# Sample attention of a hybrid decoder trunk: whole cache loads with the newest row written over the oldest

## The chip, the cores and the metric

The kernel runs on one core of one Trainium2 chip. The metric is the device time of one execution in microseconds (us), and the median of several runs is what counts. A profile of one further execution is read beside it.

## What is computed

Two layers of a decoder trunk, for a prompt of 2048 tokens and for eight sample tokens that share the weights. Each layer normalizes its input, multiplies it by one wide matrix, runs three mixers on column groups of the result, and multiplies their outputs by one output matrix:

```python
u = _rmsnorm(x, norm_w) @ w_in
...
o, k1, v1 = _swa_decode(q, k, v, kc, vc, sinks)     # the sample tokens' attention
...
y = jnp.concatenate([ya, yb, yc], axis=-1) @ w_out
return x + y
```

The change is in the attention of the sample tokens. Each of the eight tokens has a cache of the last 128 keys and values (two heads of 64), and one new key and value. It sees the newest 128 rows, so all of the cache but its oldest row, and its own:

```python
def _swa_decode(q, k, v, kc, vc, sinks):
    kk = jnp.concatenate([kc, k], axis=1)
    vv = jnp.concatenate([vc, v], axis=1)
    s = jnp.einsum('nqhgd,nkhd->nhgqk', q.reshape(N, T, HK, G, Dh), kk) * (Dh ** -0.5)
    delta = (Wc + jnp.arange(T))[:, None] - jnp.arange(Wc + T)[None, :]
    s = jnp.where((delta >= 0) & (delta < WINDOW), s, -jnp.inf)
    p = _sink_softmax(s, sinks)
    o = jnp.einsum('nhgqk,nkhd->nqhgd', p, vv)
    return o, kk[:, -Wc:], vv[:, -Wc:]
```

The caches after the step (`s_k`, `s_v`) are outputs too. Scores, softmax and the weighted sum do not depend on the order in which the 128 rows stand, if keys and values stand in the same order.

## The kernel before

The prompt is worked through in blocks of 512 tokens, four in each layer. For each block the kernel multiplies by the input matrix in column groups (`g0`, `qk`, `v`, `o`, `z`, `x0`, `x1`, `cq`, `cz`, `bz`) and, between `z` and `x0`, by the output matrix for the block before. The unit of work is a chunk: 128 rows of weights by up to 512 columns, twelve matmuls on TensorE (`multiply`, lines 511 and 513: four token tiles, three products of high and low parts). In a layer's first block the weights are loaded raw, split in two parts and written back to DRAM; in later blocks a chunk loads the two parts ready made, 512 KB in one DMA (`load_chunk`, line 469, tile `hl` from `kept`; six buffers, issued four chunks ahead). All loads and stores are issued on SyncE's queue (SP), one behind the other.

Beside the matmuls run streams, Python generators that emit their next piece of work when a planner (`pump`, with a rate for each stream and a modelled clock) lets them between two chunks. The stream `d` is the sample tokens' work. `dec_1` is its part in the second block of each layer: gates, the mLSTM update and then the attention, `dec_c`. At the last chunk of `cq` what is left of `d` is emitted at once (`drain`). The framework that builds the program then fixes each engine's order from a simulated time line and places all waits; an instruction may stand far from where the code emits it.

`dec_c` works in eleven buffers of 128 x 516 floats, of which `U` names the last six. It loads gate, queries, keys and values of the eight tokens into `U[0]`, `U[1]` and `U[2]` (lines 1557 to 1559), normalizes and rotates keys and queries (lines 1571 to 1579, results in `U[4]` and `U[5]`), and stores them to a small DRAM tile `qd` (1582, 1583). The copies of the cache to the outputs go from DRAM to DRAM (1586), and the new row behind them (1589). Then `whole` loads K: the caches of four tokens go to one buffer, with cache row on the partition, in `U[0]` and `U[1]`. Cache rows 1 to 127 come in one DMA to partitions 0 to 126 (1598), the new row from `qd` in another one to partition 127 (1599). V goes to `U[4]` and `U[5]` in the same way, at the second of the eight tokens (1614). For each token the queries are broadcast to all partitions (1603, two buffers, loaded one token ahead), GpSimd multiplies them by the keys (1617), and VectorE sums over the head (1619). The scores of all tokens are transposed on TensorE (1625), and softmax, the transposed weights (1643), the products with V (1649) and the output's transposes (1658) follow.

Of the kernel before, what the change touches and what calls it, by code (L numbers as in the profile page):

```python
# [166 lines left out]
class Build:  # L167
# [1385 lines left out]
    def dec_c(self, l, L, D):  # L1553
        nc, I, O, U = self.nc, self.I, self.O, self.U[5:]
        TT = nc.vector.tensor_tensor
        y = self.s([8, 512], "dy")
        uz = self.load_us(l, 4368, 512, U[0])
        q = self.load_us(l, 3600, 512, U[1])
        kv = self.load_us(l, 4112, 256, U[2])
        k, v = kv[:, 0:128], kv[:, 128:256]  # L1560

        def v8(ap):
            return ap.rearrange("p (h c) -> p h c", c=64)

        R = self.rope_load(self.I['rope'][SEQ].partition_broadcast(8), 8)
        yield
        tabs = self.rope_tables(R, L, 8)
        self.dec_gate(l, 4368, y, uz, U[3], True)
        rs = yield from self.qk_norm(8, [q], k.unsqueeze(1), [U[i][:8, 0:512] for i in (4, 5)])
        yield  # L1570
        TT(v8(k), v8(k), rs[:, 8:10].unsqueeze(2).to_broadcast([8, 2, 64]), op=ALU.mult)
        sc = self.s([8, 8], "dsc")
        nc.vector.tensor_scalar(sc, rs[:, 0:8], 0.125, None, op0=ALU.mult)
        TT(v8(q), v8(q), sc.unsqueeze(2).to_broadcast([8, 8, 64]), op=ALU.mult)
        tm, kr, qr = [U[i][:8] for i in (3, 4, 5)]
        self.rope(8, v8(k), tabs[1], v8(kr[:, 0:128]), 2, v8(tm[:, 0:128]), nc.vector)
        nc.vector.tensor_copy(kr[:, 128:256], v)
        yield
        self.rope(8, v8(q), tabs[0], v8(qr[:, 0:512]), 8, v8(tm[:, 0:512]), nc.vector)
        qd = self.dr.tile([8, 768], F32, name=self.nm("qd"))  # L1580
        yield
        nc.sync.dma_start(qd[:, 0:512], qr[:, 0:512])
        nc.sync.dma_start(qd[:, 512:768], kr[:, 0:256])
        cat = "b w a d -> b w (a d)"
        for cache, out in (('cache_k', 's_k'), ('cache_v', 's_v')):
            nc.sync.dma_start(O[out][l, :, 0:127].rearrange(cat), I[cache][l, :, 1:128].rearrange(cat))
        yield
        for i, out in enumerate(('s_k', 's_v')):
            nc.sync.dma_start(O[out][l, :, 127].rearrange("b a d -> b (a d)"), qd[:, 512 + 128 * i:640 + 128 * i])
        ST = self.s([128, 64], "dST")  # L1590
        Ks, Vs = U[0:2], U[4:6]

        def whole(name, x, c0):

            for i in range(2):
                bs = slice(4 * i, 4 * i + 4)
                d = x[i][:, 0:512].rearrange("p (b c) -> p b c", b=4)
                nc.sync.dma_start(d[0:127], I[name][l, bs, 1:128].rearrange("b w a d -> w b (a d)"))
                nc.sync.dma_start(d[127:128], qd[bs, c0:c0 + 128].unsqueeze(0))  # L1599

        def load(b):
            qb = U[2 + b % 2][:, 0:512]
            nc.sync.dma_start(qb, qd[b, 0:512].partition_broadcast(128))
            return qb

        whole('cache_k', Ks, 512)
        nxt = load(0)
        yield
        for b in range(8):
            qb = nxt  # L1610
            if b < 7:
                nxt = load(b + 1)
            if b == 1:
                whole('cache_v', Vs, 640)
            kb = Ks[b // 4][:, (b % 4) * 128:(b % 4) * 128 + 128].rearrange("p (a d) -> p a d", d=64)
            q4 = qb.rearrange("p (a h d) -> p a h d", a=2, d=64)
            nc.gpsimd.tensor_tensor(q4, q4, kb.unsqueeze(2).to_broadcast([128, 2, 4, 64]), op=ALU.mult)
            yield
            nc.vector.tensor_reduce(ST[:, b * 8:b * 8 + 8], v8(qb), AX.X, ALU.add)

        SK = U[0][:, 0:64]
        nc.vector.tensor_copy(SK.rearrange("p (b h) -> p b h", h=8), L['sink'].unsqueeze(1).to_broadcast([128, 8, 8]))
        yield
        ps = self.mx()
        nc.tensor.transpose(ps[:64, 0:128], ST, self.ident)
        nc.tensor.transpose(ps[:64, 128:256], SK, self.ident)
        sk = self.s([64, 1], "dsk")
        nc.vector.tensor_copy(sk, ps[:64, 128:129])
        m, nm, es, den = [self.s([64, 1], f"dsm{i}") for i in range(4)]
        nc.vector.tensor_reduce(m, ps[:64, 0:128], AX.X, ALU.max)  # L1630
        TT(m, m, sk, op=ALU.max)
        TT(es, sk, m, op=ALU.subtract)
        nc.scalar.activation(es, es, AF.Exp)
        nc.vector.tensor_scalar(nm, m, -1.0, None, op0=ALU.mult)
        P = U[2][:64, 0:128]
        nc.scalar.activation(P, ps[:64, 0:128], AF.Exp, bias=nm, accum_out=den)
        yield
        TT(den, den, es, op=ALU.add)
        nc.vector.reciprocal(den, den)
        nc.vector.tensor_scalar(P, P, den, None, op0=ALU.mult)  # L1640
        yield
        pt = self.mx()
        nc.tensor.transpose(pt[:, 0:64], P, self.ident[:64, :64])
        PT = U[3][:, 0:64]
        nc.vector.tensor_copy(PT, pt[:, 0:64])
        yield
        po = self.mx()
        for b in range(8):
            nc.tensor.matmul(po[:, b * 8:b * 8 + 8], Vs[b // 4][:, (b % 4) * 128:(b % 4) * 128 + 128], PT[:, b * 8:b * 8 + 8],
                             start=True, stop=True)  # L1650
        oS = U[3][:, 64:96].rearrange("p (h b) -> p h b", b=8)
        p4 = po[:, 0:64].rearrange("p (b a h) -> p a h b", a=2, h=4)
        nc.vector.tensor_copy(oS[0:64], p4[0:64, 0])
        nc.vector.tensor_copy(oS[64:128], p4[64:128, 1])
        yield
        pf = self.mx()
        for h in range(4):
            nc.tensor.transpose(pf[:8, h * 128:h * 128 + 128], oS[:, h, :], self.ident)
        TT(y, y, pf[:8, :], op=ALU.mult)
        yield  # L1660
        self.dec_finish(y, 2, L)
        yield
# [225 lines left out]
```

## Time and profile before

| | us |
|---|---|
| median of 3 runs (3124.88 to 3131.53) | 3127.26 |
| the profiled execution | 3129.54 |
| its span, first to last instruction | 3127.7 |
| TensorE busy in the span | 2956.6 |
| VectorE busy | 1876.9 |
| ScalarE busy | 1252.6 |
| GpSimd busy | 713.0 |

The mean granted TensorE clock is 0.976 of full speed. PE is TensorE's matmuls, PEld its weight loads, DVE VectorE, ACT ScalarE, POOL GpSimd, and SPq the issuing of DMAs on SyncE. A row of a timeline gives start and duration of an instruction; the bracket at its end is the time for which its engine stood idle before it, and what ended that.

### The profile page before, as it was taken

The numbers are of one execution on the slowest core, as the hardware profiler recorded it, in microseconds if no ns is written. First come the engines' busy times: TensorE is split into PE (matmuls) and PEld (weight loads), VectorE is DVE, ScalarE is ACT, GpSimd is POOL, SyncE is SP. The second block draws the span as 40 slices with busy tenths as digits, with TensorE's granted clock in tenths as the row PEclk, the third lists the DMA queues.
The fourth block names the chain that finished last, engine by engine and source line by source line (L and its number), as shares of the span: only waits on it lengthen the run. The fifth ranks groups of instructions, "written<-read, shape, count | busy, mean of one in ns | idle before, by whom it ended". The sixth has DMA issues, their size and how long they took to land.

```text
span 3127.7 us, 42759 instructions
## 1 busy us (share of the span) xinstructions
PE 2956.6 (95%) x14722; PEld 2420.9 (77%) x14722; DVE 1876.9 (60%) x4630; ACT 1252.6 (40%) x3080; POOL 713.0 (23%) x808
## 2 busy tenths in 40 slices
PE   6999999699999999999999999996999999999988
PEld 5787878478777788887878778874888788878877
DVE  4259656377557664467644676572765658544774
ACT  4243545124633254323554344540255324442254
POOL 3336105122012310004331561231310204000300
PEclk9999999899999999999999999997999999999999
DMA  7865548365367555564565754574544764455533
GB/s 207 279 200 188 188 148 285 117 213 177 133 194 231 160 155 164 162 191 139 174 227 181 233 198 160 194 246 163 163 151 157 241 199 151 148 160 179 163 110 127
DMA packets 263685, 567.29 MB, mean 181 GB/s; under 512 B 66900, under 2 KB 100052, under 8 KB 263420
## 3 DMA queue, kind: packets, MB, share of 16 engines
q1 hardware_dynamic: 263468, 564.56, 56.0%
q8 instruction: 116, 1.90, 0.2%
q14 instruction: 101, 0.83, 0.1%
HBM read 434.70 MB, written 132.06 MB: 181 GB/s over the span
## 4 chain that ended last, share of the span: by engine, by line
PE 73%; DVE 9%; DMA 7%; SPq 3%; issue 3%; POOL 2%; ACT 2%; DVEq 0%; POOLq 0%; ACTq 0%
PE pj L511 31%; PE pj L513 26%; DMA wr<-in_w_in 2%; PE mx L1180 2%; PE mx L1143 2%; SPq L1599 2%; PE mx L974 2%; PE mx L1171 1%; DMA hl<-kept 1%; POOL hl L491 1%; DMA kept<-hl 1%; PE mx L533 1%; PE mx L534 1%; PE mx L1221 1%; PE mx L861 1%
## 5 line engine op out<-in xcount | busy, mean ns | idle before, releaser
L513 PE MATMUL pj<-hl,xTh 128*128 128x512 f32 (+1 forms) x3072 | 958.5, 386 | 14.9 <-DVE quad L554 6.8
L511 PE MATMUL pj<-xTh,hl 128*128 128x512 f32 x2240 | 735.2, 406 | 75.0 <-DMA hl<-kept 71.8
L513 PEld LDWEIGHTS pj<-hl,xTh 128*128 128x128 f32 x3072 | 567.5, 191 | 126.1 <-DVE quad L554 8.3
L513 PE MATMUL pj<-hl,xTl 128*128 128x512 f32 (+1 forms) x1536 | 585.5, 384 | 0.0
L511 PEld LDWEIGHTS pj<-xTh,hl 128*128 128x128 f32 x2240 | 425.9, 192 | 175.7 <-DMA hl<-kept 66.7
L511 PE MATMUL pj<-parts,hl 128*128 128x512 f32 x2016 | 517.5, 404 | 11.1 <-DVE parts L1235 4.1
L511 PE MATMUL pj<-xTl,hl 128*128 128x512 f32 x1120 | 441.8, 404 | 0.0
L511 PEld LDWEIGHTS pj<-parts,hl 128*128 128x128 f32 x2016 | 368.6, 189 | 91.7 <-DVE parts L1235 5.8
L491 POOL TENSOR_TENSOR hl<-wr,hl 128x512 fp32r<-128x512 f32 (+1 forms) x208 | 279.5, 1349 | 438.6 <-ACT hl L488 383.7
L513 PEld LDWEIGHTS pj<-hl,xTl 128*128 128x128 f32 x1536 | 292.7, 191 | 52.8
L511 PEld LDWEIGHTS pj<-xTl,hl 128*128 128x128 f32 x1120 | 214.5, 192 | 44.9
L1235 DVE SCALAR_TENSOR_TENSOR parts<-quad,lp_ynw,parts 128x512 fp32r<-128x512 f32 x168 | 141.7, 845 | 162.8 <-ACT quad L1232 74.7
L488 ACT ACTIVATE hl<-wr 128x512 fp32r<-128x512 f32 (+1 forms) x208 | 126.6, 615 | 232.2 <-DMA wr<-in_w_in 76.3
L1158 ACT ACTIVATE unit<-unit,c_m,c_sc 128x256 f32<-128x256 f32 (+1 forms) x192 | 112.2, 586 | 86.2 <-DVE c_m L1149 86.1
L1174 DVE TENSOR_TENSOR parts<-mx,parts 128x512 fp32r<-128x512 f32 x124 | 84.5, 686 | 96.6 <-ACT parts L1173 94.5
L649 DVE SCALAR_TENSOR_TENSOR quad<-quad,lp_cw,quad 128x512 f32<-128x512 f32 x192 | 142.0, 784 | 0.3
L1228 ACT ACTIVATE parts<-quad,lp_ynw 128x512 fp32r<-128x512 f32 x112 | 80.6, 722 | 152.2 <-PE pj L511 142.7
L1022 POOL TENSOR_TENSOR unit<-quad,rpqn 128x256 f32<-128x256 f32 x32 | 24.1, 755 | 503.5 <-PE mx L941 225.7
L1173 ACT ACTIVATE parts<-mx 128x512 fp32r<-128x512 f32 x124 | 73.1, 595 | 106.9 <-PE mx L1171 104.6
L1180 PE MATMUL mx<-parts,vs 128*128 128x512 f32 x248 | 104.0, 435 | 6.9 <-ACT parts L1173 5.6
L393 POOL TENSOR_TENSOR quad<-quad 128x512 f32<-128x512 f32 x24 | 33.6, 1399 | 296.9 <-ACT quad L391 296.3
L805 ACT ACTIVATE unit<-quad 128x128 f32<-128x128 f32 x128 | 39.8, 311 | 138.5 <-DVE quad L863 135.8
(404 smaller groups left out, 4562.8 us busy)
## 6 DMA issues: line engine op xcount, KB each, us to landing
hl<-kept SPq DMA_DIRECT2D x576, 512.0 KB
kept<-hl SPq DMA_DIRECT2D x192, 512.0 KB
wr<-in_w_in SPq DMA_DIRECT2D x144, 256.0 KB
hl<-kept SPq DMA_DIRECT2D x48, 272.0 KB
wr<-in_w_out SPq DMA_DIRECT2D x32, 256.0 KB
quad<-in_xT SPq DMA_DIRECT2D x32, 256.0 KB
x<-quad SPq DMA_DIRECT2D x32, 256.0 KB
quad<-x SPq DMA_DIRECT2D x16, 512.0 KB
```

The costliest lines, as they stand in the source:

```text
L488: nc.scalar.activation(h, raw, AF.Copy)
L491: nc.gpsimd.tensor_tensor(lw, raw, h.bitcast(F32), op=ALU.subtract)
L511: nc.tensor.matmul(ps[t], w[:, tt], a, start=st and first, stop=en and last)
L513: nc.tensor.matmul(ps[t][:, :N], a[:, tt], w[:, :N], start=st and first, stop=en and last)
L649: nc.vector.scalar_tensor_tensor(acc, u[:, j:j + 512], cw[:, j, c:c + 1], acc, op0=ALU.mult, op1=ALU.add)
L974: nc.tensor.matmul(pY[:, h * 64:h * 64 + 64], W[h // 4][:, (h % 4) * 128:(h % 4) * 128 + 128], xdt[:, h * 64:h * 64 + 64], start=True, sto ...
L1158: nc.scalar.activation(P(a, j), P(a, j), AF.Exp, bias=nm[:, j:j + 1], scale=head(sc, a, j), accum_out=den[:, j:j + 1])
L1173: nc.scalar.activation(PTh, pT, AF.Copy)
L1174: TT(PTl, pT, PTh.bitcast(F32), op=ALU.subtract)
L1180: nc.tensor.matmul(pO[a], vs[:, x, a, :], p, start=x == 0 and i == 0, stop=x == nk - 1 and i == 1)
L1228: nc.scalar.activation(yh.rearrange("p (t c) -> p t c", c=128), pt, AF.Copy, scale=L['ynw'][:, k:k + 1])
L1235: nc.vector.scalar_tensor_tensor(yl.rearrange("p (t c) -> p t c", c=128), blk, L['ynw'][:, k:k + 1], yh.bitcast(F32).rearrange("p (t c) -> ...
```

## The change

K's load moves ahead of the copies to the outputs, V's ahead of the first query's broadcast. Each load takes all 128 cache rows to the 128 partitions. The new row is written over the oldest one, on partition 0, by a DMA of its own: for K behind the copies' new rows, for V at the fourth token.

```diff
--- before.py
+++ after.py
@@ -1581,6 +1581,21 @@
         yield
         nc.sync.dma_start(qd[:, 0:512], qr[:, 0:512])
         nc.sync.dma_start(qd[:, 512:768], kr[:, 0:256])
+        Ks, Vs = U[0:2], U[4:6]
+
+        def whole(name, x):
+
+            for i in range(2):
+                d = x[i][:, 0:512].rearrange("p (b c) -> p b c", b=4)
+                nc.sync.dma_start(d, I[name][l, 4 * i:4 * i + 4].rearrange("b w a d -> w b (a d)"))
+
+        def newest(x, c0):
+
+            for i in range(2):
+                d = x[i][0:1, 0:512].rearrange("p (b c) -> p b c", b=4)
+                nc.sync.dma_start(d, qd[4 * i:4 * i + 4, c0:c0 + 128].unsqueeze(0))
+
+        whole('cache_k', Ks)
         cat = "b w a d -> b w (a d)"
         for cache, out in (('cache_k', 's_k'), ('cache_v', 's_v')):
             nc.sync.dma_start(O[out][l, :, 0:127].rearrange(cat), I[cache][l, :, 1:128].rearrange(cat))
@@ -1588,30 +1603,22 @@
         for i, out in enumerate(('s_k', 's_v')):
             nc.sync.dma_start(O[out][l, :, 127].rearrange("b a d -> b (a d)"), qd[:, 512 + 128 * i:640 + 128 * i])
         ST = self.s([128, 64], "dST")
-        Ks, Vs = U[0:2], U[4:6]
-
-        def whole(name, x, c0):
-
-            for i in range(2):
-                bs = slice(4 * i, 4 * i + 4)
-                d = x[i][:, 0:512].rearrange("p (b c) -> p b c", b=4)
-                nc.sync.dma_start(d[0:127], I[name][l, bs, 1:128].rearrange("b w a d -> w b (a d)"))
-                nc.sync.dma_start(d[127:128], qd[bs, c0:c0 + 128].unsqueeze(0))
 
         def load(b):
             qb = U[2 + b % 2][:, 0:512]
             nc.sync.dma_start(qb, qd[b, 0:512].partition_broadcast(128))
             return qb
 
-        whole('cache_k', Ks, 512)
+        newest(Ks, 512)
+        whole('cache_v', Vs)
         nxt = load(0)
         yield
         for b in range(8):
             qb = nxt
             if b < 7:
                 nxt = load(b + 1)
-            if b == 1:
-                whole('cache_v', Vs, 640)
+            if b == 3:
+                newest(Vs, 640)
             kb = Ks[b // 4][:, (b % 4) * 128:(b % 4) * 128 + 128].rearrange("p (a d) -> p a d", d=64)
             q4 = qb.rearrange("p (a h d) -> p a h d", a=2, d=64)
             nc.gpsimd.tensor_tensor(q4, q4, kb.unsqueeze(2).to_broadcast([128, 2, 4, 64]), op=ALU.mult)
```

## Rows read from the trace of the kernel before

**Rows 1.** Page, part 1: busy us, share of the span, instructions.

```profile
PE 2956.6 (95%) x14722; PEld 2420.9 (77%) x14722; DVE 1876.9 (60%) x4630; ACT 1252.6 (40%) x3080; POOL 713.0 (23%) x808
```

**Rows 2.** Waits of all engines: who for whom, total us, times, longest.

```profile
PE pj L511 <- DMA hl<-kept: 71.8, 9, 19.3
```

**Rows 3.** Stretches: us, busy (count) PE, PEld; then clock, DMA; L511 first.

```profile
580.00:640.00 60.00, 20.19 (x61) 14.09 (x60) 0.66 0.38 124
2096.00:2180.00 84.00, 47.36 (x164) 34.70 (x163) 0.78 0.39 132
...
580.00:640.00 60.00, 22.09 (x77) 16.46 (x76) 10.71 (x17) 6.52 (x20) 11.10 (x11) 0.66 0.38 124
2096.00:2180.00 84.00, 50.15 (x197) 39.14 (x196) 23.42 (x49) 8.01 (x29) 11.35 (x13) 0.78 0.39 132
```

**Rows 4.** Chain that ended last: start us, duration us, engine, line, count.

```profile
540.40 2.78 PE pj L511 x12
...
594.65 5.49 PE pj L511 x12
...
600.63 0.87 PE mx L853 x4
...
604.30 0.91 PE mx L861 x8
```

**Rows 5.** Timeline of SP: three of eight cache loads, the issue behind each.

```profile
560.70 0.26 SPq L1598 DMA_DIRECT2D unit<-in_cache_k  x1
561.28 10.57 SPq L469 DMA_DIRECT2D hl<-kept  x1
...
594.16 0.29 SPq L1598 DMA_DIRECT2D unit<-in_cache_v  x1
594.55 14.61 SPq L469 DMA_DIRECT2D hl<-kept  x1
...
2143.39 0.28 SPq L1598 DMA_DIRECT2D unit<-in_cache_v  x1
2143.72 13.16 SPq L1599 DMA_DIRECT2D unit<-qd  x1
```

**Rows 6.** DMA view, 560 to 576 us in 40 slices: GB/s.

```profile
GB/s 0 0 0 0 8 0 19 22 22 22 22 22 22 22 22 22 22 20 20 20 22 20 20 20 20 22 20 20 20 20 22 133 154 133 174 225 351 359 425 415
```

**Rows 7.** Timeline, layer 1: SP behind the first load, TensorE's next start.

```profile
2095.97 9.89 SPq L469 DMA_DIRECT2D hl<-kept  x1
...
2111.08 1.22 PE L511 MATMUL pj<-xTh,hl 128*128 128x512 f32 x2 [5.10 <-DMA hl<-kept]
```

**Rows 8.** Timeline, SSD state: its load on SP, the product that needs it.

```profile
889.86 0.38 SPq L1512 DMA_DIRECT2D unit<-in_state_ssm  x1
...
892.79 1.30 POOL L1525 TENSOR_TENSOR unit<-unit,ddA 128x512 f32<-128x512 f32 x1 [74.06 <-DMA unit<-in_state_ssm]
```

**Rows 9.** Waits of SP for DMAs: total us, times, longest.

```profile
SPq L1512 <- DMA out_s_h<-unit: 15.8, 9, 3.0
...
SPq L1603 <- DMA unit<-qd: 6.5, 5, 2.2
```

**Rows 10.** Timeline of SP, 60 to 100 us: the first output copy.

```profile
73.53 0.84 SPq L1586 DMA_DIRECT2D out_s_k<-in_cache_k  x1
```

**Rows 11.** Rotation's end, third sample, last sum, transposes: layer 0, then layer 1.

```profile
568.93 0.68 DVE L1025 TENSOR_TENSOR unit<-unit,unit 8x512 f32<-8x512 f32 x1
...
631.86 1.26 POOL L1617 TENSOR_TENSOR unit<-unit,unit 128x512 f32<-128x512 f32 x1 [30.88 <-DMA unit<-qd]
...
655.79 0.69 DVE L1619 TENSOR_REDUCE dST<-unit 128x8 f32<-128x512 f32 x1 [1.33 <-POOL unit L1617]
...
657.35 0.11 PE mx L1625
...
2104.89 0.67 DVE L1025 TENSOR_TENSOR unit<-unit,unit 8x512 f32<-8x512 f32 x1
...
2192.30 0.11 PE mx L1625
```

## The prediction

> **What bounds the kernel now.** I read the page first: TensorE is busy for 2956.6 us of the 3127.7 us span, 95% [rows 1], so time can be won or lost only where it stands or runs slowly. The view of waits says why it stands: nine waits of an output-projection or input-projection matmul (L511) for a kept weight tile, 71.8 us in all, the longest 19.3 us [rows 2]. The table by stretches shows that they lie in two places alone: from 580 to 640 us TensorE is busy for 22.09 us, so idle 37.9, and from 2096 to 2180 us for 50.15 us of 84, so idle 33.9; together these are the 71.8 [rows 3]. The granted clock there is 0.66 and 0.78, because after each standstill TensorE runs at 1.2 GHz for a while: twelve L511 matmuls take 5.49 us behind a wait and 2.78 us otherwise [rows 4]. These two stretches are where the sample tokens' attention of layer 0 and layer 1 loads its caches.
>
> What each stretch loses, idle time and slow clock together, is its length less its matmuls at full speed. One L511 matmul is 2.78/12 = 0.232 us; an L853 matmul 0.87/4 = 0.218; the others go by L861, 0.91/8 = 0.114 [rows 4]. First stretch: 61 x 0.232 = 14.1, 4 x 0.218 and 12 x 0.114 = 2.2, so 16.4 us of work in 60: **43.6 us lost**. Second: 164 x 0.232 = 38.0, 4 x 0.218 and 29 x 0.114 = 4.2, so 42.2 of 84: **41.8 us lost** [rows 3, 4]. Sum 85.4 us.
>
> Why the weights are late is seen on SP's queue. A load of 127 cache rows is issued in 0.26 to 0.29 us, and the DMA issue right behind it then lasts 10.57, 14.61 or 13.16 us where 0.3 to 0.4 is usual; there are eight such loads (two halves of K and of V in two layers), and these are the first, one of the middle and the last [rows 5]. During the first of them the whole core moves 20 to 22 GB/s [rows 6]: 254 KB at that rate is about 12 us, the length of the stall. So a load of 127 rows uses a small part of the DMA engines, and everything behind it on SP, the weights among it, stands until it has drained. How long TensorE lives on what was fetched before: the load of layer 1 blocks SP from 2095.97, and TensorE runs dry at 2111.08 - 5.10 = 2105.98, so some 10 us of cover [rows 7].
>
> **The change, part by part.**
>
> *128 rows in place of 127, eight loads.* The kernel has a transfer of this very shape: the SSD state, 128 partitions with four runs of 512 B. It is issued in 0.38 us at 889.86, and the GpSimd product that needs it starts at 892.79 [rows 8], so it lands within 2.9 us, with no stall behind it. With that, the eight stalls go, and with them up to 85.4 us. Bytes grow by 2 KB a load, which is nothing. What the trace leaves open is only that the source is the cache and not the state; both have runs of 512 B.
>
> The Trainium skill, page "DMA: Bandwidth & Descriptors", section "Why a DMA increments its semaphore by 16 and not by 1", says that the number of engines is the largest up to 16 that divides both sides' slowest dimension, with 127 partitions giving one engine. The 20 to 22 GB/s agree; the trace doesn't name the engine. By that rule the sum is the same 85.4, and the third and fourth cases below could not happen through the loads.
>
> *The newest row written over row 0, after the load.* Before, row 127 was a partition of its own and waited for nothing but the rotated values; now four small writes a layer must wait until the load that they overwrite has landed. They are the same count and size as before, so their issue costs nothing new. The wait is new, and SP holds it: behind it stand the weight loads, the query broadcasts and the block's stores. The trace has no such wait; its nearest are SP's waits for a store before a load, 3.0 us at most, and for the rotated values, 2.2 us at most [rows 9]. From below it is nothing (the V writes come three samples after their load); from above 4 x 3.0 = 12 us a layer. Against the 10 us of cover the excess is 2 us, and a restart at the slow clock costs 5.49 - 2.78 = 2.7 us more. I take nothing, since K's two halves share one landing, and keep 0 to 4.7 us a layer.
>
> The page's section "Two DMAs through the same engine are not ordered" speaks against this part: the second write of the same bytes must await the first's completion. No run here shows an overwriting DMA. With the page's fixed cost of about 2 us for one DMA (section "Anatomy of one DMA — SWDGE (gpsimd) path", another issue path) an estimate is 8 us a layer, under the cover, and the sum would not move.
>
> *K's load ahead of the copies to the outputs, V's ahead of the queries.* The copies are issued at 73.5 us, half a millisecond before the attention [rows 10]: the order in the code does not bind them, and being behind K's load costs nothing. K's first half was already issued at 560.70, ahead of the end of the rotation [rows 5]. V's load now stands ahead of the first query; V overwrites the buffers from which the rotated values are stored, so it waits for that store, which the first query waits for as well, and then takes two issues of 0.4 us. Cost: under 1 us a layer, covered by the same 10 us.
>
> *What is late next.* When weights come on time, TensorE reaches the transposes of the scores (L1625) sooner, and the scores have their own chain: query broadcast, product on GpSimd, reduction on VectorE, eight times over two buffers. Layer 0: the rotation ends at 568.93 + 0.68 = 569.6; store and landing take up to 3.0, the first query 2.9, and the new row's wait up to 3.0. Samples 3 to 8 ran from 631.86 to 656.48, 4.1 us each; eight take 32.8. Sum 41.7 us. TensorE's work from 569.6 to L1625 at 657.35 is 87.7 - 43.6 = 44.1 us: 2.4 us to spare. In layer 1 it is from 2105.56 to 2192.30, less 41.8: 44.9 us, 3.2 to spare [rows 11]. That is little. The queue in which the broadcasts stand is fuller than before, since weights and state are fetched in half the time. I take 3 us a layer lost here, between nothing and the rival's 15.4.
>
> **Sum**: 85.4 - 2 x 3 = 79.4 us. The profiled execution took 3129.54 us, 1.84 more than its span: 3129.5 - 79.4 = 3050.1. It lies 2.3 above the median of the runs; against the median the forecast is **3048 us**.
>
> **The rivals.**
>
> 1. *The scores become the bound.* With 6 us a sample in place of 4.1 the chain is 15.2 us longer; less 2.5 to spare, plus 2.7 for the restart, 15.4 us a layer. Gain 85.4 - 31 = 54: about 3073. For: the margin is small, and broadcasts wait on SP behind weights. Against: the 4.1 us were measured while TensorE was mostly at full pace.
>
> 2. *The loads no longer stall, but the order of everything shifts.* The issue order isn't the order of the code [rows 10], so a changed wait can move work elsewhere. TensorE's idle time outside the two stretches is 3127.7 - 2956.6 - 71.8 = 99 us; a tenth of that either way is 10 us. It lies on top of each case.
>
> 3. *The change doesn't do what it says*: SP stands as long behind something else in the same stretches, and TensorE waits the same: 3127, within 6. The eight stalls all stand right behind the eight loads, which speaks against it.
>
> 4. *Slower.* If a load of 128 rows still took 10 us or more to land, SP would stand as now, and at the new row's write it would also wait for the landing, up to 3.0 us for each of eight loads: 24 us, so about 3151. The point from which this decides is a landing longer than the 10 us of cover; the state's 2.9 us [rows 8] is far below it.
>
> **How the numbers follow.** Forecast (3032 to 3060): 0.70. Rival 1 (3060 to 3090): 0.22. Rival 3: 0.03. Slower: 0.03; 0.02 for a gain between rivals 1 and 3. The range goes down to 85.4 us gained and 10 for the order, 3127.3 - 95 = 3032, and up to rival 1 with most of the 10: 3080. A difference of 0.2%, about 6 us, is what a measurement of this kernel can tell from none; by it faster is 0.94, the same 0.03, slower 0.03.
>
> **What the profile of the changed kernel would show.** The issue behind each cache load lasts under 1 us; between 20 and 22 GB/s is nowhere moved for 10 us. TensorE's waits for kept tiles fall from 71.8 us to under 10, and the two stretches (both some 40 us shorter) show a clock near 1.0. SP waits for cache_k landings show at the new row's writes, 3 us or less each. The prediction is wrong if TensorE waits at L1625 for VectorE (rival 1), if weights stay late behind the new row's writes (4), or if waits of another kind appear far from the two stretches (2).

## The result and the profile after

| | before | changed |
|---|---|---|
| median us | 3128.01 (3124.88 to 3131.53) | 3046.51 (3043.46 to 3049.93) |
| profiled execution, span | 3129.54, 3127.7 | 3047.01, 3044.9 |

The ratio is 0.9739, 95% interval 0.9723 to 0.9756: 81.5 us less, where a median of 3048 had been forecast, 80 less.

The page's first part has TensorE busy for 12 us less than in [rows 1] with the same number of matmuls, in a span that is 83 us shorter. Fewer of them run at the slow clock: the mean granted clock is 0.989 where it was 0.976.

```profile
PE 2944.7 (97%) x14722; PEld 2414.3 (79%) x14722; DVE 1873.7 (62%) x4630; ACT 1248.7 (41%) x3080; POOL 720.6 (24%) x808
```

The waits of TensorE from 550 to 700 us, all of them. The wait for kept weight tiles of [rows 2] is gone; from 2040 to 2150 us there is no wait at all. What comes late next is the first of these rows, the transposes of the scores:

```profile
PE mx L1632 <- DVE dST L1626: 1.6, 1, 1.6
PE mx L974 <- DVE unit L969: 0.5, 1, 0.5
PE pj L513 <- DVE quad L554: 0.3, 1, 0.3
```

The stretches that answer to [rows 3], all engines: TensorE is busy throughout, at full clock, and the DMA engines move 290 GB/s where it was 124 and 132:

```profile
580.00:612.00 32.00, 32.00 (x146) 26.23 (x145) 21.89 (x38) 7.52 (x23) 10.56 (x7) 1.00 0.84 290
2066.00:2104.00 38.00, 38.00 (x170) 31.03 (x169) 23.45 (x47) 7.75 (x24) 11.33 (x8) 1.00 0.86 292
```

SP's timeline shows why; these rows answer to [rows 5]. The issue behind a cache load takes 0.35 us (first half of K) or 1.55 us for two broadcasts (behind both halves of V). The GB/s from 560 to 576 us, in 40 slices, answer to [rows 6]: it nowhere stays near 20.

```profile
560.51 0.38 SPq L1590 DMA_DIRECT2D unit<-in_cache_k  x1
561.09 0.35 SPq L469 DMA_DIRECT2D hl<-kept  x1
...
575.58 0.98 SPq L1590 DMA_DIRECT2D unit<-in_cache_v  x2
576.60 1.55 SPq L1609 DMA_DIRECT2D unit<-qd  x2
```

```profile
GB/s 0 0 0 13 127 255 374 328 379 394 394 287 169 36 31 184 236 266 318 389 410 394 405 261 177 192 325 207 26 0 0 6 40 5 5 87 164 164 317 369
```

The new waits are SP's, for the landing of a load at the write of the newest row; total us, times, longest:

```profile
SPq L1596 <- DMA unit<-in_cache_v: 1.9, 2, 1.6
...
SPq L1596 <- DMA unit<-in_cache_k: 0.6, 1, 0.6
```

### The profile page after: what moved, and what is told of

Same layout as the page of the kernel before. It is cut to its first block, busy times and chain, and to the rows that moved or that the text cites. A ratio compares the mean times of both kernels' runs of the same rounds, so it can differ in the third digit from the quotient of the medians.

```text
span 3044.9 us, 42758 instructions
## 1 busy us (share of the span) xinstructions
PE 2944.7 (97%) x14722; PEld 2414.3 (79%) x14722; DVE 1873.7 (62%) x4630; ACT 1248.7 (41%) x3080; POOL 720.6 (24%) x808
## 4 chain that ended last, share of the span: by engine, by line
PE 72%; DVE 10%; DMA 7%; issue 4%; POOL 3%; ACT 2%; SPq 1%; POOLq 0%; DVEq 0%; ACTq 0%
PE pj L511 30%; PE pj L513 27%; DMA wr<-in_w_in 2%; PE mx L1180 2%; PE mx L1143 2%; PE mx L1171 1%; PE mx L974 1%; POOL hl L491 1%; PE mx L1221 1%; PE mx L840 1%; PE mx L847 1%; PE mx L534 1%; PE mx L533 1%; DVE quad L649 1%; PE mx L983 1%
## 5 line engine op out<-in xcount | busy, mean ns | idle before, releaser
L511 PE MATMUL pj<-xTh,hl 128*128 128x512 f32 x2240 | 725.0, 401 | 3.3 <-ACT xTh L1228 3.1
L511 PE MATMUL pj<-parts,hl 128*128 128x512 f32 x2016 | 517.4, 404 | 10.8 <-ACT parts L1228 3.7
L511 PEld LDWEIGHTS pj<-xTh,hl 128*128 128x128 f32 x2240 | 420.9, 189 | 98.2 <-ACT xTh L1228 4.1
L511 PEld LDWEIGHTS pj<-parts,hl 128*128 128x128 f32 x2016 | 368.8, 189 | 91.0 <-DVE parts L1235 4.4
L511 PE MATMUL pj<-xTl,hl 128*128 128x512 f32 x1120 | 437.6, 400 | 0.0
L511 PEld LDWEIGHTS pj<-xTl,hl 128*128 128x128 f32 x1120 | 212.1, 190 | 44.7
L1022 POOL TENSOR_TENSOR unit<-quad,rpqn 128x256 f32<-128x256 f32 x32 | 24.1, 753 | 500.5 <-PE mx L941 225.7
L393 POOL TENSOR_TENSOR quad<-quad 128x512 f32<-128x512 f32 x24 | 33.9, 1414 | 287.6 <-ACT quad L391 286.9
L977 POOL TENSOR_TENSOR hst<-hst,X 128x512 f32<-128x512 f32 x32 | 34.0, 1063 | 240.3 <-PE mx L955 234.5
```

The costliest lines, as they stand in the source:

```text
L511: nc.tensor.matmul(ps[t], w[:, tt], a, start=st and first, stop=en and last)
```

## Experiments

Each kernel was timed beside the kernel before on the same chip; the ratio is to that. "Longer than the changed kernel" is the median less 0.9739 of the before beside it; with the ratios' intervals of about 0.0015 either way, such a difference is good to some 5 us.

**The rows without the places.** In the kernel before, at the old places:

```diff
-                nc.sync.dma_start(d[0:127], I[name][l, bs, 1:128].rearrange("b w a d -> w b (a d)"))
-                nc.sync.dma_start(d[127:128], qd[bs, c0:c0 + 128].unsqueeze(0))
+                nc.sync.dma_start(d, I[name][l, bs].rearrange("b w a d -> w b (a d)"))
+                nc.sync.dma_start(d[0:1], qd[bs, c0:c0 + 128].unsqueeze(0))
```

> The kernel before with one part of the change: each cache load takes 128 rows, and the newest row is written over row 0 right behind its load, all at the old places. If the number of rows is what counts (theory), the issue behind each load falls from 10 to 14 us to under 1 us and the time is that of the changed kernel, 3047 us within 8; SP now waits for the landing at each new row's write, 3 us or less each, under the 10 us of cover. If the new places of the loads brought the gain (rival), the time stays near 3128. If the wait at the new row costs what it lasts, 8 x 3 = 24 us of the gain are missing: 3071.

Measured: 3050.9 us, ratio 0.974 (0.9722 to 0.9758): the whole gain. The issue behind each load lasts 0.3 to 0.7 us.

**The places without the rows.** In the changed kernel, at the new places:

```diff
-                nc.sync.dma_start(d, I[name][l, 4 * i:4 * i + 4].rearrange("b w a d -> w b (a d)"))
+                nc.sync.dma_start(d[0:127], I[name][l, 4 * i:4 * i + 4, 1:128].rearrange("b w a d -> w b (a d)"))
-                d = x[i][0:1, 0:512].rearrange("p (b c) -> p b c", b=4)
+                d = x[i][127:128, 0:512].rearrange("p (b c) -> p b c", b=4)
```

> The changed kernel with one part undone: the loads take 127 rows again and the new row goes to partition 127, without a wait, all at the new places. Theory: the eight loads still stop SP for 10 to 14 us each, so nothing is gained; the two loads of V now follow each other, and the first query's broadcast stands behind both, some 26 us late, which may cost more than before: 3110 to 3160 us. Rival (places brought the gain): 3047.

Measured: 3129.75 us, ratio 0.9991 (0.9982 to 1.0001): nothing gained, and the lateness of the first queries cost nothing beyond it. SP's timeline has the stalls as before; in layer 0 V's second load stands behind the first, and the first queries behind both:

```profile
594.71 13.72 SPq L1590 DMA_DIRECT2D unit<-in_cache_v  x2
608.47 12.56 SPq L1609 DMA_DIRECT2D unit<-qd  x2
```

So the rows carry the whole effect, and the new places carry none that can be measured, in either direction. In layer 0 of this kernel TensorE's longest wait is not for weights but for a sum of VectorE's (L402), 22.3 us; what that sum had waited for was not followed.

```profile
PE mx L861 <- DVE ss L402: 22.3, 1, 22.3
```

**127 rows in two loads.** Is it the full 128 partitions that help, the overwriting, or only that 127 is a bad count? In the kernel before, with N = 112, 122 or 124:

```diff
-                nc.sync.dma_start(d[0:127], I[name][l, bs, 1:128].rearrange("b w a d -> w b (a d)"))
+                for r0, r1 in ((0, N), (N, 127)):
+                    nc.sync.dma_start(d[r0:r1], I[name][l, bs, 1 + r0:1 + r1].rearrange("b w a d -> w b (a d)"))
```

> The kernel before, its 127 rows loaded in two DMAs, 112 rows and 15 rows; the new row still goes to partition 127 and overwrites nothing. Theory (a partition count that shares no divisor with the DMA engines is what is slow): both parts are spread, no long issue behind them, 3047 us within 10, although not one row more or less is loaded. Rival (the whole 128 partitions, or the overwriting with its wait, are needed): 3100 to 3128.

> The kernel before, its 127 rows loaded as 122 and 5 rows. 122 is twice a prime. If a load runs on as many engines, up to 16, as divide its rows (theory), the 122 rows run on two, the core moves some 40 to 44 GB/s during one, and the issue behind it lasts some 6 us; one load is under the 10 us of cover, two close together are not: 3050 to 3085 us. If any count other than a full 128 (or a multiple of 16) is as slow as 127 (rival), 3128.

> The same as 124 and 3 rows; 124 is four times a prime. Theory: four engines, some 80 to 88 GB/s, the issue behind a load lasts 3 us or less, all under the cover: 3047 us within 10. Rival (any count other than a multiple of 16 is as slow as 127): 3128.

Measured: 112 and 15 rows 3048.36 us, ratio 0.9734 (0.9719 to 0.9748), as fast as the changed kernel with the same 127 rows as before and nothing overwritten. 122 and 5 rows 3088.43, ratio 0.9855 (0.9841 to 0.987); 124 and 3 rows 3067.73, ratio 0.9784 (0.9766 to 0.9802). The last two came out above their ranges, 122 by 3 us and 124 by 11. The rates were as expected: GB/s in 40 slices, 584 to 600 us with 122 rows, then 579 to 591 us with 124 rows. Where a cache load runs alone they are 36 to 44 and 77 to 90, where one of 127 rows had 20 to 22 [rows 6]:

```profile
GB/s 220 189 128 149 277 394 394 282 73 52 42 41 40 38 38 38 36 38 38 38 40 37 38 38 37 41 42 44 44 44 44 44 44 44 115 187 218 289 379 247
```

```profile
GB/s 271 273 230 239 183 195 222 239 396 382 280 143 102 89 106 82 84 79 77 128 294 273 367 244 207 148 89 53 85 56 108 96 101 84 90 84 87 89 85 87
```

Rates of 1 to 2 to 4 for 127, 122 and 124 rows are what the rule of divisors in the Trainium skill gives ("DMA: Bandwidth & Descriptors", section "Why a DMA increments its semaphore by 16 and not by 1": the largest number up to 16 that divides the rows, so 1, 2 and 4 engines). The runs agree in rate, and the trace's semaphore records show the number as well. After at most one update close to its issue, a load of 128 rows ends with 16 further updates (562.91 to 563.31 in the changed kernel), one of 124 rows with four (592.21 to 593.18), one of 122 with two (599.85 and 600.42), and one of 127 with a single one (577.08 in the run on SP below).

The forecast price was wrong, since even short stalls cost. V's first load in layer 0 and the issue behind it, SP, 122 rows and then 124:

```profile
583.16 0.29 SPq L1599 DMA_DIRECT2D unit<-in_cache_v  x1
583.49 7.78 SPq L1600 DMA_DIRECT2D unit<-qd  x1
```

```profile
578.51 0.33 SPq L1599 DMA_DIRECT2D unit<-in_cache_v  x1
578.89 5.32 SPq L469 DMA_DIRECT2D hl<-kept  x1
```

**One narrow load.** In the changed kernel, the first half of K alone at 127 rows, in each layer:

```diff
+                r = 127 if name == 'cache_k' and i == 0 else 128
-                nc.sync.dma_start(d, I[name][l, 4 * i:4 * i + 4].rearrange("b w a d -> w b (a d)"))
+                nc.sync.dma_start(d[0:r], I[name][l, 4 * i:4 * i + 4, 128 - r:128].rearrange("b w a d -> w b (a d)"))
...
+                r = 127 if c0 == 512 and i == 0 else 0
-                d = x[i][0:1, 0:512].rearrange("p (b c) -> p b c", b=4)
+                d = x[i][r:r + 1, 0:512].rearrange("p (b c) -> p b c", b=4)
```

> The changed kernel with one load of each layer narrow again: the first half of K takes 127 rows and its new row goes to partition 127; the other three loads stay at 128 rows. If 10 us of weights fetched ahead cover one stall (theory), layer 0 loses nothing, since its first stall did not stop TensorE before, and layer 1 loses the 5.1 us of that row and some 3 us of slow clock: 3047 to 3058 us. If each stall costs its share (rival), a quarter of 85.4 us is lost: 3068.

In this kernel the keys of four tokens stand one partition off their values, so that it weights those tokens' values wrongly; the work is the same. Measured: 3067.08 us, ratio 0.9792 (0.9777 to 0.9808), 13 us longer than the changed kernel. That is above the 0 to 11 us of the theory and below the 21 us of the rival, and the cover of 10 us did not hide the stall of layer 0. It was run again with the rows in order, and with the load on another queue, beside the changed kernel:

```diff
+                if name == 'cache_k' and i == 0:
+                    nc.sync.dma_start(d[1:128], I[name][l, 0:4, 1:128].rearrange("b w a d -> w b (a d)"))
+                    continue
                 nc.sync.dma_start(d, I[name][l, 4 * i:4 * i + 4].rearrange("b w a d -> w b (a d)"))
```

> The changed kernel with one load of each layer narrow again, the first half of K: 127 rows to partitions 1 to 127, the newest row to partition 0, so that the rows stand as in the other loads. It repeats one_narrow, in which keys and values of four tokens stood in different order. From there: 12.5 us of waits for weights, about 18 us longer than the changed kernel beside it. If a stall is hidden by the weights fetched ahead, as I first held: 3 to 11 us longer.

> The same, with this one narrow load issued on ScalarE's queue; ScalarE has no other DMA near it, so that its queue does not stop. SP can issue the next seven DMAs, and the one after them waits for the narrow load's landing. If the stop of SP's queue is what costs (theory), SP stands 4 to 6 us in place of 10.5 and the kernel is 4 to 10 us longer than the changed one. If the narrow load costs by the DMA engine that it fills, whichever queue it is on (rival), it is as long as one_narrow_sp, about 18 us longer than the changed one, and the core moves 20 to 22 GB/s while it runs.

> The changed kernel itself, beside the two on the same chip, as their base: its ratio to the kernel before 0.972 to 0.976.

Measured: changed kernel 3050.43 us, ratio 0.9734 (0.972 to 0.9747); on SP 3066.36, 0.9786 (0.9765 to 0.9808), 16 us longer; on ScalarE's queue (`nc.scalar` for `nc.sync` in the added line) 3069.98, 0.9797 (0.9784 to 0.9811), 20 us longer. The first is near the 18 us forecast for it. The second lies above the theory's 4 to 10 us, and by its time it is the rival's. Its trace says otherwise, in the main. First SP's rows of the load on SP, then ScalarE's and SP's rows of the load on ScalarE's queue, then what SP waited for there from 555 to 600 us, and the GB/s from 560 to 576:

```profile
562.60 0.26 SPq L1591 DMA_DIRECT2D unit<-in_cache_k  x1
563.17 10.52 SPq L469 DMA_DIRECT2D hl<-kept  x1
```

```profile
559.88 0.52 ACTq L1591 DMA_DIRECT2D unit<-in_cache_k  x1
...
563.27 0.32 SPq L469 DMA_DIRECT2D hl<-kept  x1
563.68 2.14 SPq L306 DMA_DIRECT2D x<-quad  x3
567.40 0.28 SPq L1583 DMA_DIRECT2D qd<-unit  x1
580.23 0.38 SPq L1593 DMA_DIRECT2D unit<-in_cache_k  x1
```

```profile
SPq L1593 <- DMA unit<-in_cache_k: 12.5, 1, 12.5
```

```profile
GB/s 0 0 9 78 192 206 349 380 250 348 183 156 96 46 257 362 410 385 390 384 380 361 113 26 26 22 24 27 26 20 22 22 22 22 22 22 22 63 22 22
```

While the narrow load ran on its own queue, SP went on issuing and up to 410 GB/s were moved. The semaphore records show what the narrow load does hold up: of each DMA of 128 rows issued beside it in layer 0, 15 of 16 updates come together and the last 2.0 to 2.7 us behind them. The weight tile issued at 563.27 landed 6.5 us later, where its counterpart in the changed kernel took 5.3. So the rival's effect is there, with 1 to 2 us a tile, and is far below the loss. In return the narrow load itself took 20.3 us from issue to landing, where on SP it took 14.5. SP stopped all the same, 12.5 us where 4 to 6 had been expected, now by the wait that the forecast named: the second half of K, which shares no data with the first, waits for the first to land. In layer 1 it is the store of the new output row that waits, 11.7 us. The list of the program's waits shows how. Each DMA takes the next of eight completion counters and waits for the DMA that had it before; here the narrow load holds counter 2, and the eighth DMA behind it asks for it:

```
L469 DMA hl_5213<-kept_1495 128x1024 [waits DMAHW3_49,PE_49]
...
L1583 DMA qd_5312<-unit_91 8x256 [waits DMAHW1_49,DVE_49,Activation_49]
L1593 DMA unit_88<-in_cache_k 128x4x128 [waits DMAHW2_49,DVE_49]
```

So in these two runs the cost went with SP's stop, by an issue or by a wait. A run with the narrow load and without any stop of SP was not made.

**All eight narrow loads on ScalarE's queue.** In the kernel before, `nc.scalar.dma_start` for the loads of 127 rows.

> The kernel before with its 127-row loads issued on ScalarE's queue in place of SP's; nothing else changes. If TensorE starves because SP stands at the issue behind a load (theory), the weights are issued on time and most of the gain comes: 3047 to 3070 us, with ScalarE stopped for 10 to 14 us where it issues two loads in a row. If the weights are late because the narrow load fills the DMA engine on which a part of each weight tile runs (rival), they land late though issued on time, and the time stays at 3100 to 3128.

Measured: 3140.44 us, ratio 1.0029 (1.0019 to 1.0038), a little slower than before and outside both forecasts. It tells nothing about the queue by itself, because two other stops took the place of the first. ScalarE stood at its own next issue, and TensorE waited for its results; ScalarE's timeline, then TensorE's waits from 555 to 660 us:

```profile
582.39 10.94 ACTq L1598 DMA_DIRECT2D unit<-in_cache_v  x1
...
593.51 14.42 ACTq L1598 DMA_DIRECT2D unit<-in_cache_v  x1
```

```profile
PE mx L853 <- ACT unit L843: 12.6, 1, 12.6
...
PE mx L401 <- ACT unit L833: 8.3, 1, 8.3
```

And SP waited for the landings, as in the run above:

```profile
SPq L469 <- DMA unit<-in_cache_k: 20.6, 1, 20.6
```

In this run a narrow load stopped the queue that issued behind it, and moving it to another queue moved the stop there.

**Stop and loss together.** SP's stop is summed over the issues right behind the narrow loads (the waits for the landing in the run on ScalarE's queue); the last two rows are against the changed kernel that ran beside them:

| kernel | SP stopped, us | longer than the changed kernel, us |
|---|---|---|
| before | 93.9 | 81.5 |
| new places, 127 rows | 89.4 | 79.5 |
| 122 and 5 rows | 42.1 | 34.5 |
| 124 and 3 rows | 24.1 | 13.8 |
| one narrow load a layer, SP, first run | 20.4 | 13.1 |
| one narrow load a layer, SP | 20.6 | 15.9 |
| one narrow load a layer, ScalarE's queue | 24.2 | 19.6 |

Where most stops are longer than 5 us, some 0.6 to 0.9 of their sum comes through, and about half where most are shorter. With some 5 us of uncertainty in each loss, the small ones fix no share closely.

## Why the prediction was right, and where it was not

The mechanism held: the eight loads stopped SP, SP's stops starved TensorE, and loads of 128 rows do neither. That the sum came within 2 us is in part luck. The two stretches gave back 84.4 us where the sum, after 6 us for the scores, had 79.4, and 3.3 us were lost again far from them.

*What the stretches lose.* The kernels' transposes of the scores (L1625, L1632 after) start at 657.2 and 614.6 us in layer 0, and the kernels were 0.2 us apart ahead of the stretch (first matmul of L1429, 537.2 and 537.0): 42.4 gained where 43.6 were counted less 3 for the scores. In layer 1 they start at 2192.1 and 2106.0, less the 44.1 by which the kernels were already apart (last of L1429, 2080.4 and 2036.3): 42.0 where 41.8 were counted less 3. The count of matmuls at full speed was the right measure; idle time alone (37.9 and 33.9) would have been 12.6 us too little. Before, then after:

```profile
L1429 PE MATMUL mx<-ident,dnum x8: 270/272/273, 537.2 to 2080.4; 128*8 128x128 f32 x8
L1625 PE MATMUL mx<-ident,dST x2: 272/272/272, 657.2 to 2192.1; 128*64 128x128 f32 x2
```

```profile
L1429 PE MATMUL mx<-ident,dnum x8: 271/272/273, 537.0 to 2036.3; 128*8 128x128 f32 x8
L1632 PE MATMUL mx<-ident,dST x2: 271/285/299, 614.6 to 2106.0; 128*64 128x128 f32 x2
```

*128 rows.* Right, and the state's load was the right row: the issue behind the first load is 0.35 us, and the load lands 2.8 us after its issue, where 2.9 was read.

*The newest row's wait.* Priced at nothing, and nothing it was: 2.5 us of waits in the whole run, and the kernel whose code has that write directly behind each load is as fast. One row was misread: the 2.2 us of [rows 9] are a wait for an earlier load out of `qd`, and SP's wait for the rotated values is another row of the same view, 5.4 us at most before:

```profile
SPq L1589 <- DMA qd<-unit: 9.8, 2, 5.4
```

The sum did not rest on it, and in the changed kernel that wait is 2.1 us in layer 0. The wait that the Trainium skill asks for here ("DMA: Bandwidth & Descriptors", section "Two DMAs through the same engine are not ordered") shows as 1.6 us at most, and all of it is hidden.

*The cover of 10 us.* This step failed, though the sum did not rest on it much. It was read from one stop, of layer 1 [rows 7], and taken as there for each. One narrow load of 10.5 us a layer should have cost 3 to 11 us and cost 16, and stops of 2 to 5 us were not free. In the run on SP, layer 1 went as forecast: TensorE stood for 5.2 us, 10 us after SP's stop began. In layer 0, where no loss was forecast, it stood for 5.7 us. TensorE ran dry there at 585.0 and again at 601.0:

```profile
588.25 0.80 PE L511 MATMUL pj<-xTh,hl 128*128 128x512 f32 x1 [3.25 <-DMA hl<-kept]
...
603.46 0.50 PE L511 MATMUL pj<-xTh,hl 128*128 128x512 f32 x1 [2.48 <-DMA hl<-kept]
```

Between its first stop and 585.0, SP waited for the store of the rotated values too, 4.3 us where it is 2.1 in the changed kernel. That this second wait came before the weights had caught up is the likely reason; no run takes the two apart.

*The scores next.* Right in mechanism, a little too dear: 3 us a layer were set, it was 1.6 in layer 0 and nothing in layer 1. The margin was thinner than worked out. Rows of VectorE, GpSimd and TensorE, layer 0, answer to [rows 11]: the first two samples start at 583.70, 14 us after the rotation (568.75 + 0.68) where 9 were counted, and the eight then take 30.8 us where 32.8 were. The chain is 45.1 us for the 41.7 of the sum, and 2.4 us to spare became a wait of 1.6:

```profile
568.75 0.68 DVE L1025 TENSOR_TENSOR unit<-unit,unit 8x512 f32<-8x512 f32 x1
...
583.70 2.52 POOL L1624 TENSOR_TENSOR unit<-unit,unit 128x512 f32<-128x512 f32 x2 [8.20 <-DMA unit<-qd]
...
613.82 0.69 DVE L1626 TENSOR_REDUCE dST<-unit 128x8 f32<-128x512 f32 x1 [1.28 <-POOL unit L1624]
...
614.56 0.30 PE L1632 MATMUL mx<-ident,dST 128*64 128x128 f32 x1 [1.57 <-DVE dST L1626]
```

*The rest of the run.* The kernels are 86.1 us apart behind the second stretch and 82.8 at the end. The 3.3 us between are not in waits. From the transposes of layer 1 to the end TensorE runs the same 4590 matmuls and stands for the same 26.1 us in both; it is busy for 3.3 us more. Before, then after:

```profile
2192.10:3127.70 935.60, 909.53 (x4590) 748.79 (x4588) 581.00 (x1447) 370.45 (x927) 132.78 (x182) 0.99 0.51 163
```

```profile
2106.00:3044.90 938.90, 912.83 (x4590) 751.82 (x4588) 580.58 (x1446) 369.75 (x927) 132.59 (x182) 0.99 0.50 162
```

The clock records there account for it: 15.4 us at the lower level, 1.2 GHz, before and 22.0 after, of which half is lost, 7.7 and 11.0. Why the clock stays low for longer there, and whether it does in every run (the four of the changed kernel differ by 6.5 us), stays open.

*The rivals.* The scores as the bound: only the 1.6 us of it. A shifted order: not seen beyond those 3 us. No effect, and slower: excluded by the measured time, 81.5 us less.

## What to carry to other kernels

Look at the number of rows in a DMA's leading dimension. In this kernel loads of 128 rows, and of 112 and 15, ran without a stop; a single row less made a quarter-megabyte load some five times as long (14.7 us from issue to landing for 2.8). 112 and 15 rows did as well as 128, so a count such as 127 can be cut in two. An issue that lasts 10 us in the timeline of a DMA queue was the mark of it here, and the load to look at is the one ahead of it. Price such stops at more than half of their sum, up to nearly all of it, for whatever is issued behind them: a cover that was read from one stop was not there for the next.

## What was not expected of the hardware

A narrow load on a queue of its own let the other queue move up to 410 GB/s beside it. It took 20.3 us itself in place of 14.5, and each DMA of 128 rows beside it in layer 0 got its last sixteenth 2.0 to 2.7 us behind the rest. ScalarE, too, stands at a DMA issue behind a narrow load, 10.9 and 14.4 us, with all its arithmetic behind it.
